# Where a transformer trunk splits its operands: values, keys and queries of the stick-breaking layer moved ahead, LayerNorm's centring moved, and a strict order in Strassen's stage

## The chip, the cores and the metric

One core of one Trainium2 chip. The metric is the device time of one execution in microseconds, median over runs. The profile is of one execution; its times are microseconds from the start of its span.

## What is computed

A decoder trunk of two layers on one sequence: 512 tokens, width 2048, 16 heads of 128, four key/value groups. Layer 0 is a sparse attention with an indexer and top-k; layer 1 is the stick-breaking attention around which the change lies. Each layer ends in a LayerNorm and a gated embedding. Cut to that:

```python
def mixer_b(x, w_in, w_o, k, v):          # k, v: shared, from x @ w_kv, 4 groups
    q, gate = jnp.split(x @ w_in, [WIDTH_B], axis=-1)
    # blocks of 128 queries, z per head
    z = einsum('bqngd,bsnd->bngqs', qg, k) * HEAD_DIM ** -0.5
    log_om = where(strict, -softplus(z), 0.0)
    suffix = cumsum(log_om, reverse=True) - log_om
    a = where(strict, exp(log_sigmoid(z) + suffix), 0.0)
    o = einsum('bngqs,bsnd->bqngd', a, v)
    return (o * silu(gate)) @ w_o

for i in range(2):
    h = mixer_a(...) if i == 0 else mixer_b(...)
    x = layer_norm(ALPHA * x + h, ln_g[i], ln_b[i])
    x = x + (p[i] @ w_ple[i]) * sigmoid(x @ w_ple_gate[i])
```

## The kernel before

All matmuls are done in three products of fp32r halves: `split` (L129) makes a high part on ScalarE (ACT) and the rest as a low part on VectorE (DVE), and `mm3` (L133 to L136) multiplies high by high, high by low and low by high. So every operand of TensorE (PE), weights among them, passes one ACT and one DVE operation (both show as L111, through which every ACT and DVE call goes). Arrays lie transposed, features on the partitions, 512 tokens along the free axis.

The order of PE's instructions is as written: PE is under a manual schedule. ACT and DVE instructions are placed by a scheduler that simulates a timeline, save those issued while `pinned[0]` is true: `Paced` (L99) keeps these in program order. Weights come in as `raw` tiles (three buffers) on SyncE's DMA queue; `wh`, `wl` have three buffers, Strassen's sums `st` two, their halves `sh`, `sl` three. A queue `bg` holds small pieces of ACT and DVE work, which `pumped` (L331) issues one at a time, at every so many steps of a matmul generator, pinned.

The stages of the profiled execution: layer 0's projections and attention until about 640 us; its output product, LayerNorm and gated embedding to about 1000; then the shared keys (plain) and, to about 1236, five products by Strassen's scheme (Winograd's form, seven products for eight), one for the values `Vf` and four for the queries `F[0]` to `F[3]`. From 1236 to about 1500 come the four groups of the stick-breaking attention with the gate's product between its steps; then layer 1's output, LayerNorm and embedding, to the end.

In the Strassen stage `strassen_items` (L343) takes a unit of weights, 256 input rows by 512 columns: `prepare` reads `raw` and makes the first and third sum in `st`; then follow the second and fourth sum, and two items, each with a split of three weight quarters (`wh`, `wl`, 128x384) and a split of four sums (`sh`, `sl`, 128x512). `gemm_s` (L383) does seven products of three 128x256 matmuls for an item into seven PSUM banks; a chunk is eight units, and its banks are shifted by one from chunk to chunk. `combine` (L406) makes four quarters of the result of the seven products m1 to m7: a copy `u` of m1, c11 = m2 + u, u = m6 + u, three operations in `rest`, and three sums `onto` the quarters, in the background. `combine_last` (L430) does it for the fifth chunk in seven operations on DVE.

The stick-breaking attention (`sticks`, L215) goes over ten units (query block i, key block kb) of one group: `logits` (z by `mm3`, then Abs, Exp, Ln on ACT, a sum on DVE, a split into `s`), `weights` (products of the halves with triangular matrices `tri`, `neg` added to z, Exp, a split into `a`) and `values` (`o` by `mm3`), each one step behind the one before. Matmuls of the gate fill PE between the steps. In the first group, g = 0, the head is written out (L1288 to L1309): the splits of the first keys, of the values and of the scaled queries stand in `bg` and are issued between the gate's first steps. `gate_items` (L1129) also puts there the pieces `restore`, which split the right half of the layer's input again, and the split of query block 3. After each group the next group's query split for block 3 and four Silu follow.

In the LayerNorm (`finish_layer`, L868) the sums come first, then the mean `dm`, the variance `va`, the reciprocal root `rs` (ACT, then three DVE operations). `centre_block(n)` subtracts the mean of a block of 128 features; `normalise(n)` (L1027) multiplies by `rs`, applies scale and shift twice on ACT (to `xh`, and in place) and makes `xl` on DVE. Block 0 is centred ahead; all the others in `normalise`.

Of the kernel before, what the change touches and what calls it, by code (L numbers as in the profile page):

```python
# [77 lines left out]
def trunk_kernel(  # L78
# [249 lines left out]
    def one():  # L328
        paced(bg.popleft())

    def pumped(gen, every=1):  # L331

        for i, _ in enumerate(gen):
            if bg and i % every == 0:
                one()
            yield
# [6 lines left out]
    def strassen_items(widths, wp):  # L343
        units = [n for n in widths for _ in range(NK // 2)]

        def prepare(n):
            raw = next_raw()
            rows = n // 256
            q = raw.rearrange("p a (b n) -> p (a b) n", b=2)
            two = [q[:, i].rearrange("p (j c) -> p j c", j=rows) for i in range(4)]  # L350
            st = wp.tile([128, 4 * H], F32, name="st", tag="st", bufs=2)[:, : 2 * n]
            st = st.rearrange("p (j i c) -> p j i c", j=rows, i=4)
            dve.tensor_tensor(st[:, :, 0], two[0], two[2], ALU.add)
            dve.tensor_tensor(st[:, :, 2], two[1], two[0], ALU.subtract)
            return q, two, st

        ready = prepare(units[0])
        for u, n in enumerate(units, 1):
            q, two, st = ready
            s1, s2, s3, s4 = (st[:, :, i] for i in range(4))  # L360
            dve.tensor_tensor(s2, s1, two[1], ALU.subtract)
            dve.tensor_tensor(s4, two[3], s2, ALU.subtract)
            rows = n // 256
            for j in range(rows):
                wh = top.tile([128, 512], F32R, name="wh", tag="wh", bufs=3)
                wl = top.tile([128, 512], F32R, name="wl", tag="wl", bufs=3)
                sh = wp.tile([128, 4, 128], F32R, name="sh", tag="sh", bufs=3)
                sl = wp.tile([128, 4, 128], F32R, name="sl", tag="sl", bufs=3)
                qh, ql = (w.rearrange("p (b c) -> p b c", b=4)[:, 0:3] for w in (wh, wl))
                split(qh, ql, q[:, 1:4, j * 128 : (j + 1) * 128])  # L370
                split(sh, sl, st[:, j])
                if j == rows - 1 and u < len(units):
                    ready = prepare(units[u])
                yield [(qh[:, i], ql[:, i]) for i in range(3)] + [(sh[:, i], sl[:, i]) for i in range(4)]
# [8 lines left out]
    def gemm_s(items, C3, M):  # L383

        rows = M[0].shape[1]
        for k in range(NK // 2):
# [3 lines left out]
            for j in range(rows):  # L390
                pinned[0] = k == j == 0
                a11, a22, a12, s1, s2, s3, s4 = next(items)
                pinned[0] = False
                terms = ((a11, b11), (a12, b21), (s2, t2), (s3, t3), (s1, t1), (s4, b22), (a22, t4))
                for i, (a, b) in enumerate(terms):
                    first, final = (j == 0, j == 1) if rows == 2 else (i % 2 == 0, i % 2 == 1 or i == 6)
                    mm3(M[i][:, j], a, b, k == 0 and first, k == NK // 2 - 1 and final)
                    yield
# [7 lines left out]
    def combine(wp, M, dst):  # L406
# [14 lines left out]

        def rest():
            dve.tensor_tensor(c12, m3, c22, ALU.add)
            dve.tensor_tensor(c22, c22, c21, ALU.add)
            dve.tensor_tensor(c21, c21, m4, ALU.subtract)

        paced(rest)
        return [lambda c=c: onto(c) for c in (c12, c21, c22)]

    def combine_last(wp, M, dst):  # L430
# [6 lines left out]
        for out, a, b, op in (  # L437
# [7 lines left out]
        ):  # L445
            dve.tensor_tensor(out, a, b, op)
        pinned[0] = False

    def build_plain(k):
# [40 lines left out]

    def c3_tiles(wp, ks):
        return [tuple(wp.tile([128, 3, H], F32R, name=f"c3{s}{k}") for s in "hl") for k in ks]

# [374 lines left out]
    def finish_layer(layer, resid, last, keep, early, ahead):  # L868
# [144 lines left out]
        dve.scalar_tensor_tensor(va, qps, -1.0 / D, va, ALU.mult, ALU.subtract)  # L1013
        dve.tensor_scalar(va, va, 1.0e-5, None, ALU.add)
        act.activation(rs, va, AF.Abs_reciprocal_sqrt)
        run(second)
        centre_block(0)
        dve.tensor_tensor(sd, rs, rs, ALU.mult)
# [6 lines left out]
        gitems = plain_stream(*[(n, NK) for n in parts]).prime()  # L1025

        def normalise(n):  # L1027
            y = fblock(n)
            if n:
                centre_block(n)  # L1030
            dve.tensor_tensor(y, y, rs, ALU.mult)
            affine = dict(bias=lnc[:, 1, layer, n : n + 1], scale=lnc[:, 0, layer, n : n + 1])
# [3 lines left out]
            dve.tensor_tensor(lo, y, hi.bitcast(F32), ALU.subtract)  # L1036

        normalise(0)
        steps(fourth, 2)
# [63 lines left out]
    kitems = plain_stream((512, NK))  # L1103
    ps_ = ExitStack()
    TF, T1, C3 = [], [], []
    shared = []

    def first_sums(E8):
        shared.extend(E8)
        C3.extend(c3_tiles(ps_.enter_context(tc.tile_pool(name="sp0", bufs=1)), range(4)))  # L1110
        flat, first = (e.rearrange("p n t -> p (n t)") for e in E8)
# [17 lines left out]
    def gate_items():  # L1129
        for k, n in ((0, 8), (4, 2)):  # L1130
            yield from plain_items([(512, n)])
            raw = next_raw()
            bg.extend(lambda raw=raw, k=k: restore(raw, k) for k in range(k, k + 4))
            bg.append((lambda: split_scaled(0, 3)) if k == 0 else (lambda: split_keys(1)))
        yield from plain_items([(512, 6), *[(512, NK)] * 3])

    with ps_:
        sp = ps_.enter_context(tc.tile_pool(name="sp1", bufs=1))
        C3.extend(c3_tiles(sp, range(4, 8)))
        Kf, Vf = shared  # L1140
# [13 lines left out]
        for n, dst in enumerate((Vf, *F)):  # L1154
            M = product_banks(4 - n)
            gemm = pumped(gemm_s(items, C3, M), 8)
            if n == 1:
# [6 lines left out]
            if n == 4:  # L1164
                items = Ahead(gate_items(), 2).prime()
                combine_last(sp, M, lambda i: quarter(dst, i))
            else:
                bg.extend(combine(sp, M, lambda i: quarter(dst, i)))

    pc_ = ExitStack()  # L1170
    pc = pc_.enter_context(tc.tile_pool(name="pc", bufs=1))
    K, Q = {}, {}
    V = [tuple(pc.tile([128, 4, 128], F32R, name=f"v{s}{t}") for s in "hl") for t in range(4)]

    def split_keys(g):
        K[g] = tuple(pc.tile([128, T], F32R, name=f"k{s}", tag=f"k{s}", bufs=2) for s in "hl")
        split(*K[g], Kf[:, g])

    def split_values(t):
        split(*V[t], Vf[:, :, t * 128 : (t + 1) * 128])  # L1180

    def scaled_parts():
        return [pc.tile([128, 4, 128], F32R, name=f"q{s}", tag=f"q{s}", bufs=4) for s in "hl"]

    def split_scaled(g, i):
        qh, ql = scaled_parts()
# [3 lines left out]
        Q[i] = tuple(a.rearrange("p h q -> p (h q)") for a in (qh, ql))  # L1190
# [10 lines left out]
    px = pc_.enter_context(ss(name="px", bufs=1))  # L1201
    px_ = ExitStack()
    pa_late = []

# [10 lines left out]
    def sticks(g, Q):  # L1215
# [34 lines left out]
        def weights(u):  # L1250
# [7 lines left out]
            if kb == i:  # L1258
                strict(a)
            if u or g:  # L1260
                parts = tuple(pa_late[0].tile([128, 512], F32R, name=f"a{s}", tag=f"a{s}", bufs=2) for s in "hl")
            else:

                parts = [a.rearrange("p h q -> p (h q)") for a in scaled_parts()]
            split(*parts, a)
            state[u] = parts

        def values(u):
            i, kb = units[u]
            if kb == i:  # L1270
                out[i] = bank(7, "o")
            mm3(out[i], [v[:, g] for v in V[kb]], state.pop(u), kb == i, kb == 0)
            if kb == 0:
                act.activation(F[g][:, :, i * 128 : (i + 1) * 128], out[i].rearrange("p (h q) -> p h q", h=4), AF.Copy)

        for s in range(12):

            if s > 2 and units[s - 3][1] == 0 and g < 3:
                bg.append(lambda i=units[s - 3][0]: split_scaled(g + 1, i))
            for fn, u in ((logits, s), (weights, s - 1), (values, s - 2)):  # L1280
# [7 lines left out]
    log_exp()  # L1288
    bg.append(lambda: split_keys(0))
    bg.extend(lambda i=i: split_scaled(0, i) for i in range(2))  # L1290
    banks = mm_banks("g")
    chunk = gate_first(banks)
    gemm = pumped(chunk)
    steps(gemm, 9)
    first = sticks(0, Q)
    steps(first, 1)
    steps(gemm, 1)
    steps(first, 1)
    bg.extend(lambda i=i: split_values(i) for i in range(2))
# [29 lines left out]
    px_.close()  # L1329
    pk_.close()  # L1330
# [51 lines left out]
```

## Time and profile before

| | |
|---|---|
| median of 3 runs | 1879.36 us (1879.32 to 1879.56) |
| the profiled execution | 1879.05 us |
| its span | 1877.2 us |
| PE busy | 1868.1 us, 9229 matmuls |
| weight loads (PEld) busy | 1586.2 us |
| DVE busy | 1192.1 us |
| ACT busy | 939.2 us |
| PE's granted clock | 1.00 |
| DMA | 189.22 MB, 32.7% of the engines' time on the main queue |

Busy is the share of the span in which the profile shows an instruction on an engine. Matmul ends are modelled, so a stall of PE is best read from the starts of neighbouring matmuls. A row of the timeline reads: start, duration, engine, line, operation, tiles out<-in and shape, count, and in brackets how long the engine had been idle and what ended it.

### The profile page before, as it was taken

The page shows a single profiled execution, that of the slowest core. Times are in us where ns is not written, and L with a number is a line of the kernel's source. Part 1 is how long each engine was busy: PE and PEld are TensorE (multiplying, and loading weights), DVE is VectorE, ACT ScalarE, POOL GpSimd, SP SyncE. Part 2 cuts the span into 40 slices and gives each one's busy share as a digit, 9 for nine tenths or more (in the row PEclk, how much of TensorE's full clock was granted, in tenths as well). Part 3 has the DMA queues.
Part 4 walks back from the last instruction along what each step waited for, and adds up shares of the span by engine and source line. Part 5 has one row for each costly group of instructions (what it writes and reads, how often), then busy time and mean ns, then how long its engine had stood idle before and what let it go on. Part 6 is the DMA issues. An engine that isn't in the chain of part 4 may idle for free. (4 is left out here: it accounts for less than half of the span.)

```text
span 1877.2 us, 25016 instructions
## 1 busy us (share of the span) xinstructions
PE 1868.1 (100%) x9229; PEld 1586.2 (85%) x9229; DVE 1192.1 (64%) x2326; ACT 939.2 (50%) x1712; POOL 26.5 (1%) x46
## 2 busy tenths in 40 slices
PE   9999999999999999999999999999999999999998
PEld 8898888888888888888888999987888888888887
DVE  5768678566555455675368788867656645567534
ACT  3546333455554432474245444468877743347422
POOL 0000000000000000000000000000100000000000
PEclk9999999999999999999999999999999999999999
DMA  6442333322222532433343333322122253242333
GB/s 196 127 124 58 100 94 98 99 59 68 68 68 68 170 105 78 123 97 111 113 135 113 104 100 113 102 88 81 58 67 70 64 181 100 74 129 91 123 102 112
DMA packets 111179, 189.22 MB, mean 101 GB/s; under 512 B 8528, under 2 KB 29008, under 8 KB 111056
## 3 DMA queue, kind: packets, MB, share of 16 engines
q1 hardware_dynamic: 111056, 187.62, 32.7%
q8 instruction: 72, 1.18, 0.3%
q14 instruction: 51, 0.42, 0.1%
HBM read 179.21 MB, written 8.39 MB: 100 GB/s over the span
## 5 line engine op out<-in xcount | busy, mean ns | idle before, releaser
L111 ACT ACTIVATE wh<-raw 128x512 fp32r<-128x512 f32 (+3 forms) x685 | 397.1, 581 | 673.7 <-PE g L135 232.0
L111 DVE TENSOR_TENSOR wl<-raw,wh 128x512 fp32r<-128x512 f32 (+3 forms) x685 | 430.5, 630 | 463.1 <-ACT wh L111 449.5
L134 PE MATMUL g<-xh,wh 128*128 128x512 f32 x1024 | 403.2, 394 | 0.1
L135 PE MATMUL g<-xl,wh 128*128 128x512 f32 x1024 | 400.0, 391 | 0.4 <-DVE xl L111 0.4
L136 PE MATMUL g<-xh,wl 128*128 128x512 f32 x1024 | 399.6, 390 | 0.0
L136 PEld LDWEIGHTS g<-xh,wl 128*128 128x128 f32 x1024 | 192.2, 188 | 40.6
L135 PEld LDWEIGHTS g<-xl,wh 128*128 128x128 f32 x1024 | 192.4, 188 | 38.6 <-DVE xl L111 1.2
L134 PEld LDWEIGHTS g<-xh,wh 128*128 128x128 f32 x1024 | 192.4, 188 | 38.6 <-ACT wk L111 0.7
L135 PE MATMUL o<-xl,wh 128*128 128x512 f32 x512 | 199.2, 389 | 0.0
L136 PE MATMUL o<-xh,wl 128*128 128x512 f32 x512 | 199.2, 389 | 0.0
L134 PE MATMUL o<-xh,wh 128*128 128x512 f32 x512 | 199.2, 389 | 0.0
L136 PEld LDWEIGHTS o<-xh,wl 128*128 128x128 f32 x512 | 96.1, 188 | 20.2
L135 PEld LDWEIGHTS o<-xl,wh 128*128 128x128 f32 x512 | 96.1, 188 | 20.1
L134 PEld LDWEIGHTS o<-xh,wh 128*128 128x128 f32 x512 | 96.1, 188 | 19.9
L134 PE MATMUL q<-xh,wh 128*128 128x512 f32 x256 | 99.6, 389 | 0.0
L135 PE MATMUL q<-xl,wh 128*128 128x512 f32 x256 | 99.6, 389 | 0.0
L136 PE MATMUL q<-xh,wl 128*128 128x512 f32 x256 | 99.6, 389 | 0.0
L111 ACT ACTIVATE sh<-st 128x512 fp32r<-128x512 f32 x80 | 49.0, 628 | 80.5 <-PE m L135 43.3
L111 DVE TENSOR_TENSOR sl<-st,sh 128x512 fp32r<-128x512 f32 x80 | 54.4, 689 | 36.0 <-ACT sh L111 36.0
L111 DVE TENSOR_TENSOR xl<-f,xh 128x512 fp32r<-128x512 f32 x80 | 54.3, 686 | 11.3 <-ACT f L111 11.0
L111 ACT ACTIVATE wk<-z 128x512 f32<-128x512 f32 x80 | 47.0, 589 | 25.0 <-PE z L136 17.4
L134 PEld LDWEIGHTS q<-xh,wh 128*128 128x128 f32 x256 | 48.0, 188 | 10.1
(294 smaller groups left out, 3343.5 us busy)
## 6 DMA issues: line engine op xcount, KB each, us to landing
raw<-w_in_a SPq DMA_DIRECT2D x95, 512.0 KB, 3.7
raw<-w_in_b SPq DMA_DIRECT2D x64, 512.0 KB, 3.8
raw<-w_ple_gate SPq DMA_DIRECT2D x52, 512.0 KB, 3.7
raw<-w_o_a SPq DMA_DIRECT2D x24, 512.0 KB, 3.8
raw<-w_o_b SPq DMA_DIRECT2D x24, 512.0 KB, 3.7
raw<-w_kv_b SPq DMA_DIRECT2D x16, 512.0 KB, 3.8
raw<-w_ple_gate SPq DMA_DIRECT2D x24, 256.0 KB, 2.9
f<-xT SPq DMA_DIRECT2D x4, 1024.0 KB, 6.4
```

Source lines behind the costliest of these rows:

```text
L111: ins = method(*args, **kw)
L134: pe.matmul(out, a[0], b[0], start=start, stop=False)
L135: pe.matmul(out, a[0], b[1], start=False, stop=False)
L136: pe.matmul(out, a[1], b[0], start=False, stop=stop)
```

## The change

It has four parts, and no matmul, DMA or data operation is added or taken away.

Strassen's items are all issued pinned, that is in the written order, and not only the first of a chunk. For the second unit of each chunk `prepare` is called when its item is made instead of one item ahead, so that it stands behind the combination of the chunk before. `combine` issues only c12 at once; the sum onto c22 and c21's subtraction become pieces of the background, ahead of the three `onto`. The pieces are issued at the named steps 13, 20, 27, 34, 41 of a chunk instead of every eighth.

The splits of the values and of the first group's keys become pieces of the last Strassen chunk (steps 53, 65, 77, 89, 101). For this the three-sum tiles `C3` lie in two big tiles, and V, K, Q and A, the halves of values, keys, queries and weights, take the places (`spots`) in them that the last chunk has read; their own tiles go.

In the first group's head query blocks 0 and 1 are split behind the last operation of `combine_last`, and blocks 2 and 3 together, queued before the eight gate steps; the `drain` and two gate steps of the head go. The query splits for the next group, which in g = 0 were issued as each block ended, start at step 8 there.

In both LayerNorms blocks 0 and 1 are centred right behind the variance (`issue_after`), and both are multiplied by `rs` before block 0 is normalised.

```diff
+    def pumped_at(gen, when):
+        for i, _ in enumerate(gen):
+            if bg and i in when:
+                one()
+            yield
...
-            q, two, st = ready
+            q, two, st = ready or prepare(units[u - 1])
...
-                    ready = prepare(units[u])
+                    ready = prepare(units[u]) if u % 8 != 1 else None
...
-                pinned[0] = k == j == 0
+                pinned[0] = True
                 a11, a22, a12, s1, s2, s3, s4 = next(items)
                 pinned[0] = False
...
-        def rest():
-            dve.tensor_tensor(c12, m3, c22, ALU.add)
-            dve.tensor_tensor(c22, c22, c21, ALU.add)
-            dve.tensor_tensor(c21, c21, m4, ALU.subtract)
-
-        paced(rest)
-        return [lambda c=c: onto(c) for c in (c12, c21, c22)]
+        paced(dve.tensor_tensor, c12, m3, c22, ALU.add)
+        return [
+            lambda: dve.tensor_tensor(c22, c22, c21, ALU.add),
+            lambda: dve.tensor_tensor(c21, c21, m4, ALU.subtract),
+            *(lambda c=c: onto(c) for c in (c12, c21, c22)),
+        ]
...
-        centre_block(0)
+        with tc.issue_after(variance.ins):
+            for n in range(2):
+                centre_block(n)
...
+        def scaled(n):
+            dve.tensor_tensor(fblock(n), fblock(n), rs, ALU.mult)
+
         def normalise(n):
             y = fblock(n)
-            if n:
+            if n > 1:
                 centre_block(n)
-            dve.tensor_tensor(y, y, rs, ALU.mult)
+                scaled(n)
...
+        scaled(0)
+        scaled(1)
         normalise(0)
...
+    def c3_tiles(wp):
+        big = wp.tile([128, 24, H], F32R, name="c3")
+        spots.extend(big[:, 2 * n : 2 * n + 2].rearrange("p a t -> p (a t)") for n in range(12))
+        return [(big[:, n : n + 3], big[:, n + 3 : n + 6]) for n in range(0, 24, 6)]
...
-            bg.append((lambda: split_scaled(0, 3)) if k == 0 else (lambda: split_keys(1)))
+            if k:
+                bg.append(lambda: split_keys(1))
...
+    V, K = ([tuple(spots[n : n + 2]) for n in where] for where in ((0, 2, 4, 6), (8, 14) * 2))
+    Q, A = ([tuple(spots[n : n + 2]) for n in where] for where in ((10, 12, 16, 18), (20, 22)))
...
-            gemm = pumped(gemm_s(items, C3, M), 8)
+            gemm = pumped_at(gemm_s(items, C3, M), (13, 20, 27, 34, 41, 53, 65, 77, 89, 101))
...
+            if n == 3:
+                bg.extend(lambda t=t: split_values(t) for t in range(4))
+                bg.append(lambda: split_keys(0))
...
-            if s > 2 and units[s - 3][1] == 0 and g < 3:
-                bg.append(lambda i=units[s - 3][0]: split_scaled(g + 1, i))
+            done = [i for n, (i, kb) in enumerate(units) if kb == 0 and s == max(n + 3, 0 if g else 8)]
+            if g < 3:
+                bg.extend(lambda i=i: split_scaled(g + 1, i) for i in done)
...
-    bg.append(lambda: split_keys(0))
-    bg.extend(lambda i=i: split_scaled(0, i) for i in range(2))
+    def after_combining(fn, *args):
+        with tc.issue_after(combined):
+            fn(*args)
+
+    bg.extend(lambda i=i: after_combining(split_scaled, 0, i) for i in range(2))
...
-    steps(gemm, 9)
     first = sticks(0, Q)
-    steps(first, 1)
-    steps(gemm, 1)
-    steps(first, 1)
-    bg.extend(lambda i=i: split_values(i) for i in range(2))
+    for n in (9, 1):
+        steps(gemm, n)
+        steps(first, 1)
+    bg.extend(lambda i=i: split_scaled(0, i) for i in (2, 3))
     steps(gemm, 8)
-    drain()
-    steps(first, 1)
-    bg.extend(lambda i=i: split_values(i) for i in range(2, 4))
-    steps(gemm, 2)
-    pv_.close()
-    pa_late.append(px_.enter_context(ss(name="pal", bufs=1, side="right")))
-    bg.append(lambda: split_scaled(0, 2))
     gemm = pumped(chunk, 2)
...
-            interleave(first, 30 - 3, gemm, 64 - 20)
+            interleave(first, 30 - 2, gemm, 64 - 18)
```

More of the change, by code (lines that the diff above doesn't have):

```diff
@@ L445, in combine_last @@
         ):
-            dve.tensor_tensor(out, a, b, op)
+            last = dve.tensor_tensor(out, a, b, op)
         pinned[0] = False
+        return last.ins
     def build_plain(k):
@@ L489, in first_chunk @@
         return items
-    def c3_tiles(wp, ks):
-        return [tuple(wp.tile([128, 3, H], F32R, name=f"c3{s}{k}") for s in "hl") for k in ks]
+    spots = []
+    def c3_tiles(wp):
+        big = wp.tile([128, 24, H], F32R, name="c3")
+        spots.extend(big[:, 2 * n : 2 * n + 2].rearrange("p a t -> p (a t)") for n in range(12))
+        return [(big[:, n : n + 3], big[:, n + 3 : n + 6]) for n in range(0, 24, 6)]
     PAIRS = [n for k in range(8) for n in (k, k + 8)]
@@ L1013, in finish_layer @@
         dve.scalar_tensor_tensor(va, qps, -1.0 / D, va, ALU.mult, ALU.subtract)
-        dve.tensor_scalar(va, va, 1.0e-5, None, ALU.add)
+        variance = dve.tensor_scalar(va, va, 1.0e-5, None, ALU.add)
         act.activation(rs, va, AF.Abs_reciprocal_sqrt)
         run(second)
-        centre_block(0)
+        with tc.issue_after(variance.ins):
+            for n in range(2):
+                centre_block(n)
         dve.tensor_tensor(sd, rs, rs, ALU.mult)
@@ L1103, in trunk_kernel @@
     kitems = plain_stream((512, NK))
-    ps_ = ExitStack()
+    pc_ = ExitStack()
     TF, T1, C3 = [], [], []
@@ L1109, in first_sums @@
         shared.extend(E8)
-        C3.extend(c3_tiles(ps_.enter_context(tc.tile_pool(name="sp0", bufs=1)), range(4)))
+        C3.extend(c3_tiles(pc_.enter_context(tc.tile_pool(name="pc0", bufs=1))))
         flat, first = (e.rearrange("p n t -> p (n t)") for e in E8)
@@ L1133, in gate_items, with split_keys, split_values @@
             bg.extend(lambda raw=raw, k=k: restore(raw, k) for k in range(k, k + 4))
-            bg.append((lambda: split_scaled(0, 3)) if k == 0 else (lambda: split_keys(1)))
+            if k:
+                bg.append(lambda: split_keys(1))
         yield from plain_items([(512, 6), *[(512, NK)] * 3])
-    with ps_:
-        sp = ps_.enter_context(tc.tile_pool(name="sp1", bufs=1))
-        C3.extend(c3_tiles(sp, range(4, 8)))
+    C3.extend(c3_tiles(pc_.enter_context(tc.tile_pool(name="pc1", bufs=1))))
+    V, K = ([tuple(spots[n : n + 2]) for n in where] for where in ((0, 2, 4, 6), (8, 14) * 2))
+    Q, A = ([tuple(spots[n : n + 2]) for n in where] for where in ((10, 12, 16, 18), (20, 22)))
+    def split_keys(g):
+        split(*K[g], Kf[:, g])
+    def split_values(t):
+        split(*(v.rearrange("p (g d) -> p g d", g=4) for v in V[t]), Vf[:, :, t * 128 : (t + 1) * 128])
+    with tc.tile_pool(name="sp", bufs=1) as sp:
         Kf, Vf = shared
@@ L1165, in trunk_kernel @@
                 items = Ahead(gate_items(), 2).prime()
-                combine_last(sp, M, lambda i: quarter(dst, i))
+                combined = combine_last(sp, M, lambda i: quarter(dst, i))
             else:
                 bg.extend(combine(sp, M, lambda i: quarter(dst, i)))
[L1170 to L1183, printed above, removed]
+            if n == 3:
+                bg.extend(lambda t=t: split_values(t) for t in range(4))
+                bg.append(lambda: split_keys(0))
+    pv_.close()
+    px = pc_.enter_context(ss(name="px", bufs=1))
     def split_scaled(g, i):
-        qh, ql = scaled_parts()
+        qh, ql = (q.rearrange("p (h q) -> p h q", h=4) for q in Q[i])
         src = F[g][:, :, i * 128 : (i + 1) * 128]
@@ L1189, in split_scaled @@
         dve.scalar_tensor_tensor(ql, src, HSCALE, qh.bitcast(F32), ALU.mult, ALU.subtract)
-        Q[i] = tuple(a.rearrange("p h q -> p (h q)") for a in (qh, ql))
     def gate_first(banks):
@@ L1199, in gate_first @@
                 yield
-    px = pc_.enter_context(ss(name="px", bufs=1))
-    px_ = ExitStack()
-    pa_late = []
     def log_exp():
@@ L1259, in weights @@
                 strict(a)
[L1260 to L1264, printed above, removed]
+            parts = A[u % 2]
             split(*parts, a)
@@ L1271, in values @@
                 out[i] = bank(7, "o")
-            mm3(out[i], [v[:, g] for v in V[kb]], state.pop(u), kb == i, kb == 0)
+            mm3(out[i], [v[:, g * 128 : (g + 1) * 128] for v in V[kb]], state.pop(u), kb == i, kb == 0)
             if kb == 0:
@@ L1328, in trunk_kernel @@
             dve.tensor_tensor(F[g][:, h], F[g][:, h], sg, ALU.mult)
-    px_.close()
     pk_.close()
```

## The prediction

> **What bounds the kernel now.** I read the page first, then the list of what TensorE waited for, then the timeline around each of those waits.
>
> ```profile
> span 1877.2 us, 25016 instructions
> ...
> PE 1868.1 (100%) x9229; PEld 1586.2 (85%) x9229; DVE 1192.1 (64%) x2326; ACT 939.2 (50%) x1712; POOL 26.5 (1%) x46
> ```
>
> TensorE (PE) is busy for 1868.1 of 1877.2 us. The change adds and removes no matmul, so at most the 9.1 us in which PE stands still can be won, and VectorE (DVE, 64%) and ScalarE (ACT, 50%) count only where they make PE wait.
>
> ```profile
> PE z L134 <- ACT qh L111: 1.0, 1, 1.0
> PE z L1255 <- ACT sh L111: 0.5, 1, 0.5
> PE z L135 <- DVE ql L111: 0.4, 1, 0.4
> PE g L135 <- DVE xl L111: 0.4, 2, 0.2
> PE z L1255 <- DVE sl L111: 0.2, 1, 0.2
> ```
>
> Columns: who waited on what, us in total, times, longest. Four of the five lines lie in the first group of the stick-breaking attention, the fourth in the LayerNorms. The list leaves out waits of a quarter of a microsecond that show in PE's rows of the Strassen stage. The list counts the wait alone; what a stall costs is read from the starts of the matmuls around it, because the matmul after a wait also runs slower. Undisturbed, a 128x512 matmul starts about 0.227 us after the one before it, a 128x256 one 0.120 us.
>
> **Part 1, heads of the Strassen chunks.** Rows of DVE and PE at the first head, one later stall of the same chunk, and the last head:
>
> ```profile
> 1070.71 0.76 DVE L111 TENSOR_TENSOR st<-raw 128x256 f32<-128x256 f32 x2
> 1071.38 0.69 DVE L111 TENSOR_TENSOR E<-m,u 128x512 f32<-128x512 f32 x1
> ...
> 1072.31 0.69 DVE L111 TENSOR_TENSOR u<-m,u 128x512 f32<-128x512 f32 x1
> ...
> 1072.73 0.28 PE L136 MATMUL m<-c3h,sl 128*128 128x256 f32 x1
> 1073.05 0.39 PE L134 MATMUL m<-c3h,sh 128*128 128x256 f32 x1
> 1073.27 0.28 PE L135 MATMUL m<-c3l,sh 128*128 128x256 f32 x1
> ...
> 1077.95 0.28 PE L135 MATMUL m<-c3l,sh 128*128 128x256 f32 x1
> 1078.19 0.39 PE L136 MATMUL m<-c3h,sl 128*128 128x256 f32 x1
> 1078.41 0.28 PE L134 MATMUL m<-c3h,sh 128*128 128x256 f32 x1
> ...
> 1196.77 0.28 PE L136 MATMUL m<-c3h,sl 128*128 128x256 f32 x1
> 1197.10 0.38 PE L134 MATMUL m<-c3h,sh 128*128 128x256 f32 x1
> 1197.32 0.28 PE L135 MATMUL m<-c3l,sh 128*128 128x256 f32 x1
> ```
>
> The fourth product of a chunk may overwrite its bank only when DVE has read m6 (`u<-m,u`, started 1072.31). PE steps 0.32 instead of 0.12 us, then 0.22 instead of 0.12: 0.30 us. The last head costs the same (0.33 and 0.22 against 0.12); there are four such heads, after the first chunk, each 0.30 to 0.34. Some 5 to 6 us later the low part `sl` of an item is late: 0.24 and 0.22 against 0.12, that is 0.22 us, in three of the four chunks. Together about 1.95 us. Ahead of `u` stand two `st` sums of the next unit (0.76) and one more third sum: the scheduler put the preparation of the unit after next before the combination.
>
> After, the items are pinned in written order, the preparation of the second unit of a chunk comes behind the combination, and two of the three rest operations become background pieces. Moving the `st` pair behind `u` alone brings `u` forward by its 0.67 us and more, against the 0.20 us by which it was late; from the written order I get `u` done 0.1 to 0.2 us before it is needed. c21's subtraction and the sum onto c22 go later by some units; the products that reuse those banks come later still. So 1.95 goes, and for the thin margin I keep 0.2 us (0 if it holds; 0.8 if each of four heads still loses 0.2). **-1.75 us.**
>
> What pinning costs inside a chunk: the stage has slack on DVE.
>
> ```profile
> 1032.00:1237.00 205.00, 204.78 (x1695) 203.43 (x1694) 161.49 (x342) 93.03 (x178) 0.00 (x0) 1.00 0.35 104
> ```
>
> In this row of the windows the columns behind the stretch are PE, weight loads, DVE, ACT: DVE is busy 161.49 of 205 us. A unit (one weight load, two items of 21 matmuls, 42 x 0.120 = 5.04 us of PE) needs four `st` operations, two `wl` and two `sl`; the five background pieces of a chunk of eight units add 0.6 us each, at most two in a unit. The V splits and the first key split, five ACT and five DVE operations of 128x512, come into the last chunk at intervals of 12 products of 0.36 us, 4.3 us each: they fit beside 5.04 us per unit. Nothing added there.
>
> **Part 2, the two LayerNorms.** Here the second copy, DVE's chain and PE:
>
> ```profile
> 1698.79 0.68 DVE L111 TENSOR_TENSOR f<-f,S 128x512 f32<-128x512 f32 x1
> 1699.51 0.69 DVE L111 TENSOR_TENSOR f<-f,rs 128x512 f32<-128x512 f32 x1
> 1700.12 0.68 DVE L111 TENSOR_TENSOR xl<-f,xh 128x512 fp32r<-128x512 f32 x1
> ...
> 1700.29 0.39 PE L134 MATMUL g<-xh,wh 128*128 128x512 f32 x1
> 1700.86 0.50 PE L135 MATMUL g<-xl,wh 128*128 128x512 f32 x1 [0.18 <-DVE xl L111]
> 1701.19 0.39 PE L136 MATMUL g<-xh,wl 128*128 128x512 f32 x1
> ```
>
> The gate's first matmuls wait for `xl` of block 1: 0.57 and 0.33 against 0.227, or 0.45 us, twice (at 816.67 too): 0.90 us. Of the three DVE operations ahead the change takes the subtraction into DVE's idle time during the reciprocal root, and the multiplication before block 0's normalisation; the subtraction, its turn-round and the multiplication are 1.3 us (1698.79 to 1700.12), against a lateness of 0.34. They are charged to block 0, whose low part I still count ready over 2 us before its use. **-0.90 us**, next late is nothing within 2 us.
>
> **Part 3, the sticks' first group.** Rows of PE and of what it waited for, in two places:
>
> ```profile
> 1254.04 1.15 ACT L111 ACTIVATE vh<-E 128x512 fp32r<-128x512 f32 x2
> ...
> 1258.93 0.39 PE L1255 MATMUL z<-sl,neg 128*128 128x512 f32 x1
> 1259.84 0.50 PE L1255 MATMUL z<-sh,tri 128*128 128x512 f32 x1 [0.52 <-ACT sh L111]
> 1260.57 0.51 PE L1255 MATMUL z<-sl,tri 128*128 128x512 f32 x1 [0.23 <-DVE sl L111]
> 1260.91 0.40 PE L134 MATMUL g<-xh,wh 128*128 128x512 f32 x1
> ...
> 1274.40 0.39 PE L136 MATMUL g<-xh,wl 128*128 128x512 f32 x1
> 1275.80 0.50 PE L134 MATMUL z<-qh,kh 128*128 128x512 f32 x1 [1.01 <-ACT qh L111]
> 1276.69 0.50 PE L135 MATMUL z<-ql,kh 128*128 128x512 f32 x1 [0.39 <-DVE ql L111]
> 1277.03 0.40 PE L136 MATMUL z<-qh,kl 128*128 128x512 f32 x1
> ...
> 1275.13 0.61 ACT L111 ACTIVATE qh<-f 128x512 fp32r<-128x512 f32 x1
> ```
>
> First place: 0.91, 0.73 and 0.34 against 0.227 each, 1.30 us. ACT is behind: keys, four value splits (the last pair is the row at 1254.04, 1.15 us) and two query splits stand in the stretch in which it also makes the stick terms. Second: 1.40, 0.89 and 0.34, 1.95 us; the split of the fourth query block starts at 1275.13, behind the pieces of restored inputs. After, values and first keys are split in the last Strassen chunk, five ACT operations and five on DVE less in the head, at 0.52 us from start to start (2.6 us for ACT, against 0.68 us by which the third unit's `sh` held PE at 1259.84); and both late query splits are queued ahead of eight gate steps, done by my count about 1251, where PE asks at 1274.40 + 0.227. **-3.25 us.**
>
> What is late next there? With one gate step fewer ahead of it, the first `o` product comes three matmuls, 0.69 us, earlier.
>
> ```profile
> 1253.52 0.62 ACT L111 ACTIVATE qh<-wk 128x512 fp32r<-128x512 f32 x1
> ...
> 1255.26 0.39 PE L134 MATMUL o<-qh,vh 128*128 128x512 f32 x1
> ...
> 1236.73 0.63 ACT L111 ACTIVATE wh<-raw 128x512 fp32r<-128x512 f32 x1
> ...
> 1238.71 0.39 PE L134 MATMUL g<-xh,wh 128*128 128x512 f32 x1
> ```
>
> The row at 1253.52 is the high part of the first weights. In the new order an exponential stands ahead of it (one ACT step, 0.52 us later, less the splits that have gone): I put its start at 1253.85, its end at 1254.47, and the low part behind it (0.69 on DVE) at 1255.2. Its matmul is the second of `o`, then due at 1254.57 + 0.227 = 1254.80. **+0.56 us** with the slow restart of 0.11, between 0 (ACT gets ahead by the splits) and 1.0.
>
> At the last combination DVE now meets the split of a gate weight before c21. The high part starts at 1236.73 and ends at 1237.36; `wl` (0.61 to the next start) and c21 (0.69) end at 1238.66 to 1238.75, and the row at 1238.71 is the first matmul into the bank that c21 frees. **+0.16**, between 0 and 0.3. The Trainium skill ("TensorE: Matmul & The Clock Gate", section "Architectural detail") has VectorE and ScalarE as strict first-in-first-out queues, so c21 cannot pass the `wl` that waits for ACT; were it able to, this term would be 0 and the sum 0.16 lower. No run here shows yet which.
>
> Finally three query splits for the next group, which used to be spread, are bunched at the ninth step: ACT and DVE then finish a unit's low part about when PE wants it. **+0.1**, 0 to 0.5. DMA queues and PE's own order keep their sequence but for the moved gate steps; the wait of 0.39 us at the first group's end keeps its cause (Silu behind a key split) and stays.
>
> **Sum.** -1.75 - 0.90 - 3.25 + 0.56 + 0.16 + 0.1 = -5.08 us. The profiled execution took 1879.05 us (1.85 outside the span), so 1873.97; it lies 0.31 under the median of 1879.36, and from the median it is 1874.3, which I forecast.
>
> **Rivals.** (A) New waits take back more: all four upper bounds together, 0.8 + 1.0 + 0.3 + 0.5 = 2.6 us against a gross 6.1, leave -3.5: 1875.9. For it speaks that three of the margins are 0.2 us or less; against it, that they are separate places. (B) Slower: strict order makes DVE the bound of the Strassen stage. By full durations a unit costs DVE two `sl` (0.69), two `wl` (0.55) and four `st` (0.42), 4.2 us, and two background pieces of 0.69 bring it to 5.5 against 5.04; were 40 units each 0.2 us late, +8, less the 4.15 of parts 2 and 3: 1883. It decides from 5.04 us per unit on. Against it: 161.49 of 205 busy, and start-to-start times are shorter than durations (0.61 for 0.69). (C) The change does only part of what it says: the sticks' head stays late because ACT, not the order, is its bound; parts 1 and 2 alone give -2.65: 1876.7.
>
> **Chances.** About 0.2% (3.76 us) is what a measurement of this kernel tells from no change. Forecast 0.72, A 0.13, C 0.07, B 0.08. The forecast's own spread, 1873.2 with every new wait at 0 to 1875.6, lies on the faster side nearly whole; A and C count as the same. The range, 1872.9 to 1877.0, takes in the forecast, A and C and leaves out B.
>
> **What would show it.** In the profile after: steps of 0.12 us across the fourth product of each chunk; the wait list without `xl` and without the 1.0 us `qh`; a new short wait of `o` on the low part of the first weights near 1252 us; PE busy unchanged near 1868 us, and the span near 1872.1. Wrong would be: units of the Strassen stage longer than 5.04 us, DVE near full there, or the head's waits back under other names.

## The result and the profile after

The changed kernel takes 1873.73 us (median of 7 runs, 1873.46 to 1874.29) against 1879.36 (median of 7 runs, 1879.26 to 1881.40): ratio 0.9968, 95% interval 0.9956 to 0.9980. The forecast was 1874.3. The profiled execution took 1873.84 us with a span of 1872.1, 5.1 us less than before (5.6 by the medians).

From the page of the changed kernel, the span, the busy times of the engines, then the list of PE's waits (us in total, times, longest):

```profile
span 1872.1 us, 24902 instructions
...
PE 1865.3 (100%) x9229; PEld 1586.2 (85%) x9229; DVE 1195.8 (64%) x2326; ACT 940.6 (50%) x1712; POOL 26.7 (1%) x46
```

```profile
PE spun L156 <- DVE xl L111: 1.4, 1, 1.4
PE o L135 <- DVE c L111: 0.2, 1, 0.2
PE z L1270 <- DVE sl L111: 0.2, 1, 0.2
```

The five waits shown of before are gone; two of 0.2 us are new. (`c` is now the name of everything that lies in the two big tiles: the three-sum halves, values, keys, queries and weights.)

The head of the second Strassen chunk, DVE and PE:

```profile
1071.23 0.68 DVE L111 TENSOR_TENSOR E<-m,u 128x512 f32<-128x512 f32 x1
1072.01 0.69 DVE L111 TENSOR_TENSOR u<-m,u 128x512 f32<-128x512 f32 x1
1072.62 0.68 DVE L111 TENSOR_TENSOR E<-m,E 128x512 f32<-128x512 f32 x1
1073.22 0.75 DVE L111 TENSOR_TENSOR st<-raw 128x256 f32<-128x256 f32 x2
...
1072.88 0.28 PE L136 MATMUL m<-c,sl 128*128 128x256 f32 x1
1073.00 0.28 PE L134 MATMUL m<-c,sh 128*128 128x256 f32 x1
1073.12 0.28 PE L135 MATMUL m<-c,sh 128*128 128x256 f32 x1
```

The two `st` sums now stand behind `u`, which ends at 1072.70, 0.3 us before the matmul that needs its bank; PE goes on at 0.120 us where before it stepped 0.32 and 0.22.

The second LayerNorm, DVE, with block 1's low part (the second `xl`):

```profile
1686.59 1.29 DVE L111 TENSOR_TENSOR f<-f,rs 128x512 f32<-128x512 f32 x2
...
1690.08 0.69 DVE L111 TENSOR_TENSOR xl<-f,xh 128x512 fp32r<-128x512 f32 x1 [1.35 <-ACT f L111]
...
1692.50 0.69 DVE L111 TENSOR_TENSOR xl<-f,xh 128x512 fp32r<-128x512 f32 x1 [0.49 <-ACT f L111]
```

Both blocks are multiplied by `rs` at once, and block 1's `xl` is ready at 1693.2. The list of waits has no `xl` of a LayerNorm left.

The new waits in the sticks' first group: `o` on the low part of the first weights, and the restart behind the last combination. Rows of ACT, DVE and PE:

```profile
1251.89 0.62 ACT L111 ACTIVATE wk<-wk 128x512 f32<-128x512 f32 x1
1252.41 0.62 ACT L111 ACTIVATE c<-wk 128x512 fp32r<-128x512 f32 x1
...
1253.07 0.69 DVE L111 TENSOR_TENSOR c<-wk,c 128x512 fp32r<-128x512 f32 x1 [0.35 <-ACT c L111]
...
1253.11 0.47 PE L134 MATMUL o<-c,c 128*128 128x512 f32 x1
1253.82 0.50 PE L135 MATMUL o<-c,c 128*128 128x512 f32 x1 [0.23 <-DVE c L111]
1254.15 0.40 PE L136 MATMUL o<-c,c 128*128 128x512 f32 x1
```

```profile
1235.70 0.69 DVE L111 TENSOR_TENSOR wl<-raw,wh 128x512 fp32r<-128x512 f32 x1 [0.43 <-ACT wh L111]
1236.31 0.68 DVE L111 TENSOR_TENSOR f<-m,u 128x512 f32<-128x512 f32 x1
...
1236.80 0.39 PE L136 MATMUL g<-xh,wl 128*128 128x512 f32 x1
1237.14 0.47 PE L134 MATMUL g<-xh,wh 128*128 128x512 f32 x1
1237.45 0.40 PE L135 MATMUL g<-xl,wh 128*128 128x512 f32 x1
```

The first costs 0.71 and 0.33 against 0.227 twice, 0.59 us: an exponential stands at 1251.89, the high part behind it, as counted. The second costs 0.34 and 0.31, 0.20 us: DVE waits for `wh` and makes `wl` before c21. The other wait on the list is of unit 6, the first unit of query block 3:

```profile
1277.36 1.02 POOL L1228 TENSOR_SCALAR_AFFINE_SELECT run<-run 128x512 f32<-128x512 f32 x1 [11.88 <-DVE run L111]
...
1278.48 0.62 ACT L111 ACTIVATE sh<-run 128x512 fp32r<-128x512 f32 x1
...
1279.22 0.69 DVE L111 TENSOR_TENSOR sl<-run,sh 128x512 fp32r<-128x512 f32 x1
...
1279.34 0.40 PE L1270 MATMUL z<-sh,tri 128*128 128x512 f32 x1
1279.96 0.50 PE L1270 MATMUL z<-sl,tri 128*128 128x512 f32 x1 [0.23 <-DVE sl L111]
1280.30 0.40 PE L134 MATMUL g<-xh,wh 128*128 128x512 f32 x1
```

0.62 and 0.34 against 0.227: 0.51 us. The chain runs from GpSimd's mask over ACT to DVE with nothing between.

### The profile page after: what moved, and what is told of

Its sections match the earlier page's. It is cut to its first block, busy times and chain, and to the rows that moved or that the text cites. A ratio compares the mean times of both kernels' runs of the same rounds, so it can differ in the third digit from the quotient of the medians.

```text
span 1872.1 us, 24902 instructions
## 1 busy us (share of the span) xinstructions
PE 1865.3 (100%) x9229; PEld 1586.2 (85%) x9229; DVE 1195.8 (64%) x2326; ACT 940.6 (50%) x1712; POOL 26.7 (1%) x46
## 4 chain that ended last, share of the span: by engine, by line
PE 99%; ACT 0%; DVE 0%; issue 0%; ACTq 0%
PE g L134 12%; PE g L135 12%; PE g L136 12%; PE o L135 7%; PE o L136 7%; PE o L134 7%; PE m L134 4%; PE m L136 4%; PE m L135 4%; PE q L134 3%; PE q L135 3%; PE q L136 3%; PE k L136 2%; PE k L135 2%; PE k L134 2%; PE z L1270 2%
## 5 line engine op out<-in xcount | busy, mean ns | idle before, releaser
L136 PEld LDWEIGHTS q<-xh,wl 128*128 128x128 f32 x256 | 48.1, 188 | 10.0
```

What stands on the lines that cost most here:

```text
L136: pe.matmul(out, a[1], b[0], start=False, stop=stop)
```

## The experiments

Each kernel ran beside the kernel before, and the ratio with its 95% interval is to that; spans are of the profiled execution. A span alone tells little below half a microsecond: over the thirteen profiles the start of PE's 41st matmul, ahead of every edit, lies between 11.7 and 12.5 us (11.88 before, 12.43 in the changed kernel). So the steps between matmuls decide.

**The Strassen edits alone.** On the kernel before:

```diff
-                pinned[0] = k == j == 0
+                pinned[0] = True
...
-                    ready = prepare(units[u])
+                    ready = prepare(units[u]) if u % 8 != 1 else None
```

with `ready or prepare(...)`, the shortened `combine` and the named steps.

> The kernel before with the Strassen edits alone (items pinned, preparation of each chunk's second unit deferred, two rest operations in the background at the named steps). Theory: the late reads of m6 and the late sl go, 1.95 us, and nothing else moves: span 1875.2, time about 1877.4, the stalls of 1.30 and 1.95 us in the sticks' head unchanged. Rival: what is won comes back as a wait further on, because ACT and DVE, not PE, set the sticks' head: span 1877.2, and the head's stalls larger by up to 1.95 us.

Span 1876.0, time 1877.49 (10 runs; 0.9988, 0.9978 to 0.9997). Nothing is left of the steps at the heads or of the late `sl` (a step of 0.18 at the third chunk's head remains, and four of 0.20 in the second chunk, which every kernel here has), and the two stalls of the sticks' head are there, 1.30 and 2.07 us. The median is 2.3 us below the 1879.78 of the kernel before beside it; the span only 1.2 below that shown before, as the two profiles differ by 0.3 us in their first 60 us, by 0.2 in the first LayerNorm's stage and by 0.1 in the second stall, places the edit does not touch. The theory holds; the rival (all of it given back) does not.

**The strict order alone.** Only `pinned[0] = True`.

> The kernel before with the strict order alone: every Strassen item pinned, the preparation, the rest operations and the background pieces as before. Theory: order without the deferral leaves the two st sums ahead of the read of m6, so the four heads keep 0.3 us each or more and no unit becomes longer than 5.04 us: span 1876 to 1878. Rival (strict order makes DVE the bound): 40 units 0.2 us longer each, span about 1885. Second rival (pinning does all of the gain): span 1875.2.

Time 1879.87 (10 runs; 1.0002, 0.9992 to 1.0011); span 1880.0, of which 1.6 us are another thing (the last section). All four heads stall, and the list of waits has one line for them:

```profile
PE m L134 <- DVE u L111: 0.7, 4, 0.2
```

By the starts the stage loses 2.36 us there, where the kernel before loses 1.95 with its late `sl`. No unit but those four is longer than in the kernel before (5.04 us, and up to 5.47 in the second chunk, alike in both): neither does order alone gain, nor is DVE the bound, and the slower rival of the prediction falls.

**Without the deferral.** The changed kernel with `q, two, st = ready` and `ready = prepare(units[u])` as before.

> The changed kernel with the preparation of each chunk's second unit put back one item ahead, all else as changed. Theory: the deferral is what brings the read of m6 forward, so the four heads lose 0.3 us each again, 1.2 us in all, span about 1873.3. Rival: the strict order and the shorter combination do it alone, span 1872.1.

Span 1874.6, time 1876.16 (10 runs; 0.9979, 0.9970 to 0.9989). DVE and PE at the second chunk's head:

```profile
1071.37 0.76 DVE L111 TENSOR_TENSOR st<-raw 128x256 f32<-128x256 f32 x2
1072.04 0.68 DVE L111 TENSOR_TENSOR E<-m,u 128x512 f32<-128x512 f32 x1
1072.83 0.69 DVE L111 TENSOR_TENSOR u<-m,u 128x512 f32<-128x512 f32 x1
```

`u` is 0.82 us later than with the deferral, and the heads lose 2.36 us, more than the 1.2 expected, since c11 (`E<-m,u`) is late as well, and just as much as with the strict order alone. So without the deferral nothing of the Strassen gain is left; the rival falls. Whether the deferral would do it without the strict order was not tried.

**The combination's rest together.** The changed kernel with `rest` as before.

> The changed kernel with the three rest operations of the combination together again, as before, order and deferral as changed. Theory: with the deferral alone the read of m6 is early, but the two more operations (1.2 us on DVE) stand ahead of the second unit's sums and its sl, so that each of the four heads loses 0.2 to 0.5 us there: span 1873 to 1874. Rival: there is slack for them, span 1872.1.

Span 1872.2, time 1873.91 (one run). Three of the four heads have slack; only the one behind the chunk with the value transposes loses 0.5 us. Mostly the rival: the shortened combination is worth 0.5 us, not 0.8 to 2. That the span comes out as the rival's is chance: this profile was 0.5 us ahead at its start, and it does not have the 0.20 us at c21, because here `wl` follows c21.

**The LayerNorm edits alone**, on the kernel before.

> The kernel before with the LayerNorm edits alone. Theory: the two waits of PE for xl of block 1 go (0.45 us each), span 1876.3, Strassen and sticks as in the profile before. Rival: the chain only moves to block 2, whose xl is then late by 0.3 us or more in each layer: span 1876.9 to 1877.2.

Both waits of `xl` are gone from the list of waits and nothing of block 2 came in their place. The span is 1878.2 (one run, 1879.94), 1.0 above before, not 0.9 below: this execution has 1.8 us more at 1275 to 1282, where no edit lies (last section). Without these it is 1876.4. The waits decide for the theory; the time of this one run tells nothing.

**Values and first keys back in the head.** On the changed kernel:

```diff
-                bg.extend(lambda t=t: split_values(t) for t in range(4))
-                bg.append(lambda: split_keys(0))
...
+    bg.append(lambda: split_keys(0))
     bg.extend(lambda i=i: after_combining(split_scaled, 0, i) for i in range(2))
...
     bg.extend(lambda i=i: split_scaled(0, i) for i in (2, 3))
+    bg.extend(lambda i=i: split_values(i) for i in range(4))
```

> The changed kernel with the splits of the values and of the first keys back in the sticks' first group (keys with the first query blocks, values behind query blocks 2 and 3 in the eight gate steps), all else as changed. Theory: ten operations of ACT and DVE come back into the head, the third unit's stick terms are late again: a stall of 0.7 to 2 us between 1249 and 1262, the 1.95 us wait for the fourth query block stays away, span 1873 to 1874. Rival (the head was late by its order, not by ACT's load): no stall over 0.6 us there, span 1872.1.

Span 1877.3, time 1879.36 (10 runs; 0.9997, 0.9988 to 1.0007). The list of waits and ACT's rows ahead of it:

```profile
PE z L1269 <- ACT sh L111: 3.8, 1, 3.8
```

```profile
1244.30 0.63 ACT L111 ACTIVATE wh<-raw 128x512 fp32r<-128x512 f32 x1 [3.45 <-PE g L135]
1244.84 2.18 ACT L111 ACTIVATE c<-E 128x512 fp32r<-128x512 f32 x4
1247.02 0.63 ACT L111 ACTIVATE wh<-raw 128x512 fp32r<-128x512 f32 x1
1248.10 0.60 ACT L111 ACTIVATE wk<-z 128x512 f32<-128x512 f32 x1 [0.45 <-DVE c L111]
```

PE steps 4.22 and 0.81 us where 0.227 is undisturbed, over the 2 us expected, and it is another stall: it falls on the first unit's `sh` (at 1252.40), and the third unit's (at 1263.36) is not late. The four value splits stand ahead of the first unit's first operation (1248.10, in the changed kernel 1242.25), all behind a split of a gate weight for which ACT stood idle for 3.45 us. So where the splits stand makes this stall; that ACT's load makes the one of 1.30 us, against the rival, this run does not show. For the load speaks the kernel before itself: ahead of the late `sh` ACT is busy for 8.32 of 8.65 us (the fourth number behind the comma), 2.3 us of it with the value splits.

```profile
1250.50:1259.15 8.65, 8.65 (x39) 6.88 (x37) 7.10 (x11) 8.32 (x18) 1.13 (x2) 1.00 0.20 68
```

**The fourth query block's split late.** On the changed kernel, block 3 goes back behind the first four restored inputs.

> The changed kernel with the split of the fourth query block back behind the first restored inputs, all else as changed. Theory: PE waits for its high and low part near 1271 to 1273 again, 1 to 2 us, the earlier stall of 1.30 us stays away: span 1873 to 1874. Rival: with the value splits gone ACT has time to make it, span 1872.1 (or below, if the second query pair so early costs something).

Here the theory fell. Span 1870.9, time 1872.63 (4 runs; 0.9962, 0.9948 to 0.9977): no wait for the split, and the waits of `o` and of unit 6 are gone as well (by the starts, 0.15 us of `o`'s is left). ACT now makes the high part of the first weights (`c<-wk`) ahead of the exponential and not behind it:

```profile
1251.59 0.62 ACT L111 ACTIVATE c<-wk 128x512 fp32r<-128x512 f32 x1
1252.12 1.28 ACT L111 ACTIVATE wk<-wk 128x512 f32<-128x512 f32 x2
```

**The same split early, in the kernel before.** `bg.append(lambda: split_scaled(0, 3))` ahead of the four `restore` pieces:

> The kernel before with one piece moved: the split of the fourth query block stands ahead of the four pieces of restored inputs instead of behind them. Theory now: the wait of 1.40 and 0.89 us for that split goes (1.95 us, span 1875.3) and with it the stretch of eight matmuls at half clock that a slightly longer wait left in the profiles of two kernels (1.6 us), so no execution lies more than 1 us above the median, where the kernel before has one in five 1.5 to 2 us above its fastest. Rival: ACT is full there, the wait turns up at another matmul, span 1876.5 or more, and the late executions stay.

Span 1875.0, time 1877.60 (11 runs; 0.9986, 0.9977 to 0.9995). The wait of 1.95 us is gone; the stall of 1.31 us for the third unit stays.

With the kernel before and the changed one this makes a table of four, PE's loss in us for the third unit's `sh` and for query block 3 (the rows differ by all the other edits too):

| | block 3 split late | block 3 split early |
|---|---|---|
| head as before, values in it | 1.30 and 1.95 (before) | 1.31 and 0 |
| head as changed, values in the last chunk | 0 and 0 | 0 and 0, but 0.59 and 0.51 new (after) |

The third unit's wait goes with the changed head, whose edits (values, keys, order of the first splits) were not tried one by one, and not with block 3's place. Block 3's wait goes with either; done together, the early place is not needed and costs the two new waits.

**The first value product later.** On the changed kernel:

```diff
     steps(gemm, 8)
+    steps(first, 1)
+    steps(gemm, 2)
     gemm = pumped(chunk, 2)
...
-            interleave(first, 30 - 2, gemm, 64 - 18)
+            interleave(first, 30 - 3, gemm, 64 - 20)
```

> The changed kernel with two gate steps back between the first weights and the third logits, as in the kernel before, so that the first value product comes 0.68 us later. Theory: the new wait of o for the low part of the first weights (0.71 and 0.33 us where 0.227 is undisturbed, 0.59 us) goes, span 1871.5. Rival: the low part is made late by as much, because ACT's order follows, and the wait stays: span 1872.1.

Span 1870.9 (one run, 1872.66). The wait of `o` goes, and that of unit 6 with it, as its matmuls too come three matmuls later: 1.1 us for one move. (This profile is also 0.4 us ahead of the changed kernel's at its start.)

**The second group's keys later.** `split_keys(1)` from `gate_items` to step 8 of the first group:

> The changed kernel with the split of the second group's keys taken from behind the restored inputs and put at the ninth step of the first group. The wait of z for sl at 1279.96 (0.62 and 0.34 us, 0.50 us lost) is put down to this split, which now comes 8.6 us earlier than before and stands ahead of the unit's exponential on ACT, so that its sum meets another DVE operation while GpSimd masks it (1.02 us against 0.64 before). Theory: that wait goes, span 1871.6. Rival: the three query splits bunched at the ninth step are its cause, or the mask is slow whatever stands beside it: the wait stays, span 1872.1 or more.

Span 1872.0 (one run, 1873.78). The wait at 1279.96 goes, and the mask shrinks:

```profile
1276.36 0.64 POOL L1226 TENSOR_SCALAR_AFFINE_SELECT run<-run 128x512 f32<-128x512 f32 x1 [10.80 <-DVE run L111]
```

Without the key split ahead of its exponential it starts 1.0 us earlier, and it takes 0.64 us for 1.02. But a wait of 0.35 us appears at a later unit of query block 3, on the `sl` of these rows of DVE and PE:

```profile
1293.76 0.68 DVE L111 SCALAR_TENSOR_TENSOR c<-f,c 128x512 fp32r<-128x512 f32 x1
1294.36 0.69 DVE L111 TENSOR_TENSOR c<-wk,c 128x512 fp32r<-128x512 f32 x1
1294.96 0.69 DVE L111 TENSOR_TENSOR sl<-wk,sh 128x512 fp32r<-128x512 f32 x1
...
1295.24 0.39 PE L1268 MATMUL z<-sh,tri 128*128 128x512 f32 x1
1295.70 0.50 PE L1268 MATMUL z<-sl,tri 128*128 128x512 f32 x1
```

A split of the bunched queries (`c<-f,c`) stands ahead of it, and the key split ahead of those. So the key split's place is shown to make the wait at 1279.96, the bunched queries cost where the key split joins them, and the move gains little by itself.

**All that was left.** The changed kernel with the gate steps of the experiment before last, with

```diff
-    for n in (9, 1):
+    pinned[0] = True
+    steps(gemm, 1)
+    pinned[0] = False
+    for n in (8, 1):
```

and the third and fourth group's key splits appended at `s == 1` of their group's `sticks` instead of ahead of it.

> The changed kernel with the two gate steps back ahead of the third logits (as tried before: span 1870.9), the third gate weight's halves kept behind the last combination (the restart of 0.345 and 0.31 us at 1237.1 should go, 0.2 us), and the splits of the third and fourth group's keys moved from the group's first gate step behind its first weights, so that they no longer stand ahead of the last Silu (0.49 and 0.34 us at 1366.7, 0.38 us). Theory: span 1870.3, time about 1872.1, 0.39% under the kernel before. Rival: the moved operations make new waits of the same size, span 1870.9 or more.

Span 1870.0, time 1871.81 (5 runs, 1871.46 to 1871.96; 0.9956, 0.9942 to 0.9970): 1.9 us below the changed kernel's median (its profile is 0.4 us ahead at the start). Its list of PE's waits has one line, the start of the kernel:

```profile
PE spun L156 <- DVE xl L111: 1.4, 1, 1.4
```

## Why the prediction held, and where it did not

The time was 0.6 us off, and the terms stand so, in us:

| term | predicted | measured |
|---|---|---|
| Strassen heads and late `sl` | -1.75 | -1.95 |
| LayerNorms | -0.90 | -0.90 |
| sticks' head, both stalls | -3.25 | -3.25 |
| `o` on the first weights | +0.56 | +0.59 |
| c21 behind `wl` | +0.16 | +0.20 |
| a low part late | +0.1 | +0.51 |

They add to -4.8 of the 5.1 us by which the spans differ. The remaining 0.3 is two things that the prediction did not have. Ahead of the first LayerNorm, where no edit lies, this profile is 0.6 us behind, 0.54 of it by 8.7 us from the start. And the stick-breaking stage gains 0.9 us outside the stalls named. About 0.8 of that lies in some 140 matmuls of `o`: the start behind each comes 233 ns after its own in the kernel before and in the four kernels that leave this stage's tiles as they were, and 227 ns in the eight that have the halves in the big tiles. Why is open. So that the sum of -5.08 came so near the 5.04 of the spans is in part luck: 0.5 of new waits too few and 0.9 of gain not seen, against 0.2 of margin not needed and 0.6 at the start. The 0.2 us kept for the heads' thin margin was not needed in the changed kernel; that the margin is thin is shown by the rest put together, which loses 0.5 us at one head.

`o`: the number and the row were right, an exponential ahead of the high part; but it stands there only where block 3 is split early, as the experiment with that split late shows, and the prediction did not count this as a cost of the early split.

c21: the `wl` that waits for ACT holds it; DVE stands idle for 0.43 us ahead of that `wl`, with c21 behind it, and where `wl` comes behind c21 (in the last experiment, and with the rest together) the step at that bank is 0.227 us again. This agrees with the rule of the Trainium skill named in the prediction.

The step that failed is the last term, and in its mechanism: I put it to three query splits bunched at the ninth step. The late low part is that of unit 6, and putting off the second group's key split removes it; the change brings that split forward, from 1282.85 to 1274.20 (4.3 us of it are the lead of the whole kernel there), in part because block 3's split has left the queue ahead of it: put back, it has the key split at 1276.28. Its matmuls also come three earlier than in the kernel before, and three more ahead of them take the wait away as well (the first value product later): it takes both. Behind the bunched queries the changed kernel has no listed wait, and 0.35 us where the keys join them. I had followed the pieces that the diff names, and not the one that moves up in the queue because another has left it.

The second failure gave the right number for too broad a reason. I credited the 1.95 us to queueing block 3's split early; the runs show that it would have gone with the rest of the changed head alone. It did not touch the sum. That the 1.30 us went because ACT had less to do stays argued, from how full ACT was before.

One sentence was wrong in its frame: that at most the 9.1 us in which PE stands still could be won. PE's busy time fell by 2.8 us although no matmul went and the idle time by only 2.3 (9.1 to 6.8). A 128x512 matmul is drawn 0.39 us long and starts every 0.227, so a delay below 0.16 us, and that much of each longer one, is hidden in the overlap. The starts of neighbouring matmuls, from which the terms were made, are the measure.

Of the rivals, new waits did come, for 1.3 of the 2.6 us priced; slower by strict order and a head that stays late did not. (The upper end of the forecast's spread, 1875.6, and rival A's 1875.9 are the same sum, counted once from the profiled execution and once from the median.)

## What to carry to other kernels

When an engine is busy all the time, sum the excess of start-to-start times at each stall, and price a reordering as what goes less what comes: the old stalls were 6.1 us, the new ones 1.3, and two of the three could be named from the written order. Of two edits that may remove the same wait, try each without the other; here the second cost 1.1 us. A piece that leaves a queue brings all behind it forward, so look at these as well.

## What the runs showed of the hardware

A wait of PE can cost more than its length. In the profile of the strict order alone the wait for block 3 was 0.19 us longer than in that of the kernel before, and then:

```profile
1277.01 0.50 PE L134 MATMUL z<-qh,kh 128*128 128x512 f32 x1 [1.21 <-ACT qh L111]
1277.90 0.50 PE L135 MATMUL z<-ql,kh 128*128 128x512 f32 x1 [0.39 <-DVE ql L111]
1278.24 0.45 PE L136 MATMUL z<-qh,kl 128*128 128x512 f32 x1
1278.48 0.63 PE L134 MATMUL g<-xh,wh 128*128 128x512 f32 x1
1278.91 0.63 PE L135 MATMUL g<-xl,wh 128*128 128x512 f32 x1
...
1281.47 0.58 PE L1255 MATMUL z<-rl,neg 128*128 128x512 f32 x1
1281.89 0.39 PE L1255 MATMUL z<-sh,tri 128*128 128x512 f32 x1
```

and the windows around it (us, busy PE, PEld, DVE, ACT, POOL, then the granted clock):

```profile
1277.00:1278.50 1.50, 1.10 (x4) 0.68 (x5) 0.84 (x2) 0.00 (x0) 0.00 (x0) 0.98 0.61 218
1278.50:1282.30 3.80, 3.80 (x11) 3.02 (x10) 1.60 (x3) 2.69 (x5) 0.00 (x0) 0.56 0.01 4
```

Eight matmuls from 1278.48 to 1281.89 start 0.427 us apart instead of 0.227, at half clock, for 3.4 us: 1.6 us lost on top of 2.1 for the wait. The profile of the LayerNorm edits alone has the same at the same place, and that with values back in the head after its 4.2 us wait; in all three the granted clock is 0.50 for 3.41 us (1278.45 to 1281.86 here) and 1.00 around it. With the Strassen edits alone PE stood idle for 1.13 and 0.39 us there, against 1.21 and 0.39 in the two that dip there, and the clock stayed at 1.00. Four profiles do not make a threshold of this. Of 25 executions of the kernel before beside the first four experiments five lie between 1880.9 and 1881.4 us, the rest at or below 1880.6; with block 3's split early, which takes this wait away, all 11 lie within 0.8 us of their median. That the dips make the late executions fits, but no profile of the kernel before caught one. The Trainium skill ("TensorE: Matmul & The Clock Gate", Part 1) has the clock halve after an idle window of about 3.4 us; the length of the dip, 3.41 us, is that of one such window, but it came here after two waits of 1.2 and 0.4 us with a matmul between, well under a whole idle window.

GpSimd's mask of 128x512 took 1.02 us where DVE made a low part from two tiles beside it (in the changed kernel, DVE from 1277.21 to 1277.89), and 0.64 with the second group's keys later, where DVE stood still until 1276.82. This holds throughout: in the thirteen profiles all 47 masks of `run` that begin inside such an operation of DVE take 1.02 to 1.03 us, and the other 57, some with one that begins 0.31 us or more after them, 0.63 to 0.64.
